# The down projection of a hybrid decoder block: weight operands streamed, their sums formed during gate and up, and a new order at the entry

## The chip, the cores and the metric

The program runs on one core of one Trainium2 chip, whose engines are TensorE (PE, its weight loads PEld), VectorE (DVE), ScalarE (ACT), GpSimd (POOL) and the DMA queues of SyncE (SP) and POOL. The metric is the device time of one execution in microseconds (us). The kernel before takes 1651.36 us, the median of three runs (1650.76 to 1653.76).

## The reference

One decoder block on a sequence of 1024 tokens of 1024 channels, float32. An attention branch and a retention branch read the same normed input, are merged by gates and projected; then a SwiGLU feed-forward with 2816 hidden channels. The change is in the feed-forward part:

```python
        mixed = jnp.sum(gates * u, axis=2).astype(x.dtype)
        x = x + jnp.einsum('bsd,de->bse', mixed, w_out[l])
        h = rms_norm(x, norm2_g[l])
        ff = jax.nn.silu(h @ ffn_w_gate[l]) * (h @ ffn_w_up[l])
        x = x + ff @ ffn_w_down[l]
```

## The kernel before, in words

**Arithmetic.** A matrix product is made in float32r from operands split into a high half (a copy by ACT, `ac`) and a low half (the rest, one subtraction on DVE, `tt`): three matmuls of 128x512 instead of one, high by high, high by low, low by high. `split`, `fill` and `d_fill` write such a pair.

**Seven products.** Gate and up (`ffn1`, line 1627) and down (`ffn2`, line 1855) are Winograd's form of Strassen's scheme: each operand is cut in 2x2 blocks, sums of blocks are formed, and seven block products, numbered 1 to 7, take the place of eight. In gate and up the moving side are the activations (`H`, and their three sums, split by `s_split` into `sh`), and the stationary side is one of 22 column blocks `f` of the weights G and U and their sums (`sums` and `late` in `fw_ops`, tiles `T`); a product `prod` is 12 matmuls. `SEQ` is the order of the 154 products. Their operands lie in 12 slots (`op_ring`), each freed by its product.

**Down.** Products 2, 1, 5, 6, 3, 7, 4 (`PLAN`) each run over 11 rows `k` of blocks, 12 matmuls a row, 924 in all. A-blocks are the feed-forward's activations, which gate and up write to memory, `f_scr`, one tensor for each `f` (`z3`, line 1703); B-blocks are rows of `ffn_w_down`. `d_first` (line 1760) loads: the two streams of product 2 go through a ring of six buffers (`st_ring`), the other six block matrices are loaded whole ("quads", `d_quad`) and stay. `d_s1`, `d_s2` and `d_ops` form eight sums of two SBUF tiles for each `k`, 88 in all, each by `both`: on POOL or on DVE, whichever the planner expects to end first. The split pairs go through a ring of eight operands (`dop_ring`), four rows' worth. `d_post` adds a product's bank to the residual.

**The entry.** Between the output projection and gate and up, `out_post` (line 1383) normalises each of eight token tiles `t`, transposes it on PE into two `psT` banks, and `h2_second` makes from these the split activations and the sums `sx`, for t from 4 to 7. `psT` is also the bank of product 5 (`z_ring2`).

**Order.** All of it is written as generators. A planner (`Sched.run`, line 168) takes step by step the instruction that could start first by its own cost figures, so each engine's queue is fixed when the program is built, and each queue runs strictly in order. A `Wait` of a generator holds back only its own later instructions.

Of the kernel before, what the change touches and what calls it, by code (L numbers as in the profile page):

```python
# [16 lines left out]
T = 1024  # L17
# [66 lines left out]
class Ring:  # L84
# [20 lines left out]
    def release(self, t):  # L105
        for e in self.live:
            if e[0] is t:
                e[1] = True
                return
        raise ValueError("not live")  # L110
# [101 lines left out]
def kernel(  # L212
# [1016 lines left out]
    big = es.enter_context(tc.tile_pool(name="big", bufs=1))  # L1229
# [153 lines left out]
    def out_post(t, o):  # L1383
# [17 lines left out]
        ps = []  # L1401
        for half in range(2):
            p = yield Alloc(t_ring)
# [6 lines left out]
        if t >= 4:  # L1410
            sch.spawn(h2_second(t, *ps), 1)
# [9 lines left out]
    def h2_second(t, p0, p1):  # L1421
# [8 lines left out]
        fl.add(("A2", 0, t))  # L1430
        yield Wait(lambda: all(("A1", half, t - 4) in fl for half in range(2)))
# [4 lines left out]
        t_ring.release(p0)  # L1436
        fl.add(("S", 1, t))
        yield from split(H[:, 0, t, 4:8, :], H[:, 1, t, 4:8, :], p1v)
        t_ring.release(p1)
# [25 lines left out]
    SEQ = [(1, 0), (2, 0), (1, 1), (2, 1), (5, 0), (6, 0), (6, 1), (7, 0), (5, 1), (4, 0), (3, 0), (7, 1)]  # L1465
# [23 lines left out]
    def op_views():  # L1489
# [15 lines left out]
        return Ring([wh(n) for n in range(4)] + [new(n) for n in range(8)], True)  # L1505
# [4 lines left out]
    def fw_ops():  # L1510
# [27 lines left out]
        def sums(f):  # L1538
            yield Wait(lambda: "fe" in fl and ("hx", NT - 1) in fl and ("G", f) in fl and ("U", f) in fl)
            if f == 1:  # L1540
                yield Wait(lambda: ("S", 0, NT - 1) in fl)
            G, U = fe["G", f][0], fe["U", f][0]
            a = yield Alloc(fe["T"])
            yield either(f)(a, U[:, 0:4], G[:, 0:4], ALU.subtract)
            b = yield Alloc(fe["T"])
            yield either(f)(b, U[:, 4:8], a, ALU.subtract)
            AB[f] = a, b
# [10 lines left out]
        AB = {}  # L1558
        for p, f in SEQ:
# [7 lines left out]
            if p in (5, 6) and f not in AB:  # L1567
                yield from sums(f)
            if p == 5:
                yield from put(f, 5, AB[f][0], lambda a=AB[f][0]: fe["T"].release(a))  # L1570
            elif p == 6:
                yield from put(f, 6, AB[f][1])
                sch.spawn(late(f, G, AB[f][1]), 2)
            elif p == 7:
                c = yield Alloc(fe["T"])
                yield either(f)(c, U[:, 4:8], U[:, 0:4], ALU.subtract)
                yield from put(f, 7, c, lambda c=c: fe["T"].release(c))
            elif p == 4:
                yield Wait(lambda: f in T4)
                yield from put(f, 4, T4[f], lambda f=f: fe["T"].release(T4[f]))  # L1580
            else:
                yield from put(f, 3, U[:, 4:8], drop("U", f))

# [84 lines left out]
    def c11(f, X):  # L1668
        yield Wait(lambda: ("y1", f) in fl and ("hx", NT - 1) in fl)
# [52 lines left out]
    KH = NF // 2  # L1722
    LAST = 3
    PLAN = [(2, "V"), (1, "Y"), (5, "V"), (6, "Y"), (3, "V"), (7, "Y"), (4, "V")]
    SRC = {1: ("A11", "B11"), 5: ("A21", None), 6: ("A11", "B11"), 3: (None, "B22"), 7: (None, "B12"), 4: ("A22", None)}
# [8 lines left out]
    def both(*a):  # L1734
        return Any(tt(*a, gp), tt(*a))

    def d_of(q, k):

        f, c = (int(q[2]) - 1 if q[0] == "A" else int(q[1]) - 1) * KH + k, int(q[1] if q[0] == "A" else q[2]) - 1
        c = slice(c * 512, c * 512 + 512)  # L1740
        return f_scr[f][:, c] if q[0] == "A" else ffn_w_down[0][f * 128:(f + 1) * 128, c]

    def st_make(n):
        def make():
            if n < 4:
                return flat(f2["raw"][n // 2])[:, n % 2 * 512:n % 2 * 512 + 512]
# [3 lines left out]
    def dop_make(n):  # L1750
        def make():
            if n < 4:
                return flat(f2["hl"][n // 2])[:, n % 2 * 1024:n % 2 * 1024 + 1024].rearrange("p (s t) -> p s t", s=2)
            return f2["op", n][:, 0:2]
# [5 lines left out]
    def d_first():  # L1760
        yield Wait(lambda: n_op[0] == 7 * NF and all((L1, p) in ops for p in (5, 6, 7)))
        f2["raw"] = [(yield Alloc(raw_ring)), (yield Alloc(raw_ring))]
        for k in range(2):
            yield from d_stream(2, k, "A12", gp)
            yield from d_stream(2, k, "B21", gp)
        for n, t in enumerate(fe["h"]):
            yield Wait(lambda: n_use[0] >= 7 * NF // 12 * 12 + 2 * n + 2)
            hl_ring.release(t)
# [228 lines left out]
```

## Time and profile before

| | us |
|---|---|
| three runs, median (lowest to highest) | 1651.36 (1650.76 to 1653.76) |
| the profiled execution | 1653.68 |
| its span, first to last instruction | 1652.0 |
| PE busy in the span | 1593.2 (96%) |
| DVE, ACT, POOL busy | 1067.0 (65%), 695.8 (42%), 321.3 (19%) |
| mean granted TensorE clock | 0.983 of full speed |

The profile is of one execution. PE is the engine whose idle time counts: the chain of work that ended last is PE for 75% of the span. Its idle time is short in sum, and lies in a few places; so the views to read are those that show a stretch of time, and not the sums over the span. Line 264 is the helper of every matmul, 284 of every ACT instruction, 294 of every two-operand DVE or POOL instruction, 318 of SP's DMAs and 317 of POOL's.

### The profile page before, as it was taken

The numbers are of one execution on the slowest core, as the hardware profiler recorded it, in microseconds if no ns is written. First come the engines' busy times: TensorE is split into PE (matmuls) and PEld (weight loads), VectorE is DVE, ScalarE is ACT, GpSimd is POOL, SyncE is SP. The second block draws the span as 40 slices with busy tenths as digits, with TensorE's granted clock in tenths as the row PEclk, the third lists the DMA queues.
The fourth block names the chain that finished last, engine by engine and source line by source line (L and its number), as shares of the span: only waits on it lengthen the run. The fifth ranks groups of instructions, "written<-read, shape, count | busy, mean of one in ns | idle before, by whom it ended". The sixth has DMA issues, their size and how long they took to land.

```text
span 1652.0 us, 23325 instructions
## 1 busy us (share of the span) xinstructions
PE 1593.2 (96%) x8404; PEld 1364.8 (83%) x8404; DVE 1067.0 (65%) x2681; ACT 695.8 (42%) x1413; POOL 321.3 (19%) x325
## 2 busy tenths in 40 slices
PE   7999999999999999999999998999999999897999
PEld 7999888888888888888888877888888888675887
DVE  7566578888779886524346578544455443498785
ACT  5233367666565565223115335333333332332442
POOL 2011212221103120000000002322332221036261
PEclk8999999999999999999999999999999999998999
DMA  6564221211421210233344323222222221882122
GB/s 181 139 179 132 62 61 59 65 42 42 114 75 52 55 49 23 62 108 115 109 130 137 112 87 90 94 85 88 80 88 77 85 69 51 304 314 71 32 90 83
DMA packets 158036, 160.71 MB, mean 97 GB/s; under 512 B 18400, under 2 KB 115680, under 8 KB 157664
## 3 DMA queue, kind: packets, MB, share of 16 engines
q1 hardware_dynamic: 152672, 147.68, 28.1%
q0 software_dynamic: 5248, 11.54, 2.5%
q8 instruction: 66, 1.08, 0.3%
q14 instruction: 50, 0.41, 0.1%
HBM read 120.38 MB, written 38.81 MB: 96 GB/s over the span
## 4 chain that ended last, share of the span: by engine, by line
PE 75%; DVE 6%; DMA 4%; issue 2%; POOL 1%; ACT 1%; SPq 0%; POOLq 0%; DVEq 0%; ACTq 0%
PE psF L264 25%; PE psS L264 23%; PE psO L264 12%; PE psT L264 11%; PE psT L269 4%; DVE P L1011 1%; PE psF L269 1%; DVE wh L294 1%; DVE P L299 1%; DVE pc L294 0%; DMA B__13707<-in_ffn_w_down_dram 0%; DMA B__13703<-in_ffn_w_down_dram 0%; DMA A__13653<-f_scr 0%; DVE sh L294 0%; DMA B__13711<-in_ffn_w_down_dram 0%
## 5 line engine op out<-in xcount | busy, mean ns | idle before, releaser
L264 PE MATMUL psF<-H,wh 128*128 128x512 f32 x1056 | 278.1, 396 | 2.1 <-ACT aw L284 2.1
L264 PEld LDWEIGHTS psF<-H,wh 128*128 128x128 f32 x1056 | 194.1, 189 | 36.6 <-ACT aw L284 2.5
L264 PE MATMUL psS<-H,zh 128*128 128x512 f32 x480 | 135.1, 405 | 0.3 <-ACT zs L284 0.3
L284 ACT ACTIVATE P<-P,pm 128x640 f32<-128x640 f32 (+7 forms) x128 | 93.9, 734 | 65.7 <-DVE pm L1011 64.4
L294 DVE TENSOR_TENSOR pT<-psT,pT 128x512 fp32r<-128x512 f32 (+1 forms) x152 | 92.4, 615 | 32.6 <-ACT pT L284 32.1
L284 ACT ACTIVATE pT<-psT 128x512 fp32r<-128x512 f32 (+1 forms) x152 | 79.0, 537 | 69.3 <-PE psT L269 68.7
L264 PE MATMUL psS<-kT,qt 128*128 128x384 f32 (+3 forms) x384 | 103.0, 343 | 1.9 <-DVE pm L1011 1.8
L294 POOL TENSOR_TENSOR T<-wraw 128x512 f32<-128x512 f32 x19 | 28.9, 1522 | 389.2 <-DVE op L294 389.2
L264 PEld LDWEIGHTS psS<-H,zh 128*128 128x128 f32 x480 | 85.9, 188 | 15.1 <-ACT zs L284 0.6
L264 PE MATMUL psO<-pT,vv 128*128 128x256 f32 x528 | 91.4, 289 | 3.7 <-DVE pT L294 3.6
L264 PE MATMUL psS<-whA,H 128*128 128x256 f32 (+1 forms) x672 | 91.7, 294 | 0.2 <-POOL whA L294 0.2
L284 ACT ACTIVATE wh<-wraw 128x1024 fp32r<-128x1024 f32 (+1 forms) x60 | 50.0, 841 | 97.4 <-PE psO L264 76.8
L264 PEld LDWEIGHTS psO<-pT,vv 128*128 128x128 f32 x528 | 79.5, 189 | 12.6 <-DVE pT L294 5.5
L294 DVE TENSOR_TENSOR wh<-wraw,wh 128x1024 fp32r<-128x1024 f32 (+1 forms) x60 | 60.7, 1016 | 42.0 <-ACT wh L284 40.7
L264 PEld LDWEIGHTS psS<-whA,H 128*128 128x128 f32 x672 | 87.1, 196 | 0.4 <-POOL whA L294 0.4
L294 DVE TENSOR_TENSOR op<-T,op 128x512 fp32r<-128x512 f32 x61 | 62.7, 1029 | 27.8 <-ACT op L284 27.4
L269 PE MATMUL psT<-ident,P 128*128 128x128 f32 x528 | 79.7, 273 | 0.1
L264 PEld LDWEIGHTS psS<-kT,qt 128*128 128x128 f32 x384 | 65.3, 189 | 10.2 <-DVE pm L1011 2.6
L264 PE MATMUL psS<-yt,wh 128*128 128x512 f32 x288 | 66.6, 389 | 0.0
L264 PE MATMUL psF<-sh,op 128*128 128x512 f32 x276 | 66.0, 389 | 0.0
L269 PEld LDWEIGHTS psT<-ident,P 128*128 128x128 f32 x528 | 61.9, 140 | 4.9 <-DVE P L299 0.8
L264 PE MATMUL psS<-wh 128*128 128x512 f32 x198 | 53.2, 409 | 11.7 <-DVE wh L294 11.4
(594 smaller groups left out, 3521.4 us busy)
## 6 DMA issues: line engine op xcount, KB each, us to landing
wraw<-in_w_in_dram SPq DMA_DIRECT2D x22, 512.0 KB, 4.1
f_scr<-fs SPq DMA_DIRECT2D x22, 512.0 KB, 2.6
qt<-q_scr POOLq DMA_DIRECT2D x16, 512.0 KB, 4.1
wraw<-in_ffn_w_gate_dram SPq DMA_DIRECT2D x12, 512.0 KB, 3.8
xx<-in_ffn_w_up_dram SPq DMA_DIRECT2D x12, 512.0 KB, 3.6
rawA<-in_w_in_dram SPq DMA_DIRECT2D x20, 256.0 KB, 3.5
zr<-in_w_in_dram SPq DMA_DIRECT2D x20, 256.0 KB, 3.4
z_scr<-zs SPq DMA_DIRECT2D x20, 256.0 KB, 2.1
```

Of the source, the lines that this page charges most:

```text
L264: lambda: pe.matmul(o, l, r, start=start, stop=stop, skip_group_check=True))
L269: return Op("pe", 109, 100, [o], [i], lambda: pe.transpose(o, i, ident))
L284: return Op("act", c, 150, outs, ins, lambda: act.activation(o, i, func, scale=scale, **kw))
L294: return vop(o, [a, b], lambda: (eng or dve).tensor_tensor(o, a, b, op), eng)
L299: return vop(o, ins, lambda: (eng or dve).tensor_scalar(o, a, s1, None, op0=op0), eng, fast)
L1011: lambda: dve.tensor_tensor_reduce(o, a, b, -sc, init, ALU.add, ALU.min, acc))
```

## The change

The helper lines move by 26. In words:

- **Sums in gate and up.** `wd_sums` loads, during gate and up, two rows of `ffn_w_down` at a time into a tile `row` (two DMAs of 512 KB on POOL's queue), forms the four sums T1 to T4 of the weight blocks in place on DVE (a wait counts the products done, `n_use`), and stores them to a scratch tensor `t_scr` in memory (two DMAs of 512 KB on POOL's queue). Eleven times. `row` takes the space of two of the twelve operand slots; ten stay in use after product 12 (`Slots`).
- **Streams.** In down all B operands, raw or summed, and A12 come through a ring of 24 buffers; only A11, A21 and A22 are loaded whole. The first four rows are loaded by POOL's queue while gate and up run. No sum in down goes to POOL; 44 sums are left there, all on DVE.
- **Operand ring.** Down's ring has ten operands (five rows), and they are gate and up's own slots: operand `n` may be filled once product 145 + n of 154 is done. For that the pool `big` is kept alive on the other side of SBUF.
- **Entry.** The last token tile is transposed into a `psS` and the `psO` bank; `h2_second` of t = 6 waits after its first part until t = 7 is normed; the sums of a column block are spawned apart; `c11` waits for ("sh", 0); product (5, 1) stands before (6, 1).

```diff
+class Slots(Ring):
+    def can(self):
+        return self.slot(self.n) not in self.held
...
-    big = es.enter_context(tc.tile_pool(name="big", bufs=1))
+    big = ctx.enter_context(tc.tile_pool(name="big", bufs=1, side="right"))
...
+        ring = t_ring if t < NT - 1 else ps_ring("SO")
         for half in range(2):
-            p = yield Alloc(t_ring)
+            p = yield Alloc(ring)
...
         fl.add(("A2", 0, t))
+        yield Wait(lambda: t != NT - 2 or ("hx", NT - 1) in fl)
         yield Wait(lambda: all(("A1", half, t - 4) in fl for half in range(2)))
         yield tt(s2, s1v, s3, ALU.subtract)
...
-        return Ring([wh(n) for n in range(4)] + [new(n) for n in range(8)], True)
+        return Slots([wh(n) for n in range(4)] + [new(n) for n in range(8)],
+                     lambda n: n if n < 12 else (0, 1, 2, 3, 6, 7, 8, 9, 10, 11)[(n - 12) % 10])
...
+    def wd_sums():
+        yield Wait(lambda: n_use[0] >= 12)
+        row = fe["pool"].tile([128, 4, 512], F32, name="row", tag="op")
+        a, b, c, d = [row[:, i] for i in range(4)]
+        for k in range(KH):
+            yield Wait(lambda: n_use[0] >= 12 + 13 * k)
+            for i in range(2):
+                f = i * KH + k
+                yield dma(row[:, 2 * i:2 * i + 2].rearrange("p a n -> p (a n)"),
+                          ffn_w_down[0][f * 128:(f + 1) * 128, :], gp)
+            for i, (o, x, y) in enumerate(((a, b, a), (b, d, b), (d, d, a), (c, c, d))):
+                yield Wait(lambda: n_use[0] >= 18 + i + 13 * k)
+                yield tt(o, x, y, ALU.subtract)
+            for i in range(2):
+                yield dma(t_scr[k][i], row[:, 2 * i:2 * i + 2].rearrange("p a n -> p (a n)"), gp)
+        fl.add("ts")
...
-        yield Wait(lambda: ("y1", f) in fl and ("hx", NT - 1) in fl)
+        yield Wait(lambda: ("y1", f) in fl and ("sh", 0) in fl)
...
-    st_ring = Ring([st_make(n) for n in range(6)], True)
-    dop_ring = Ring([dop_make(n) for n in range(8)], True)
+    st_ring = Ring([st_make(n) for n in range(NST)], True)
+    dop_ring = Ring([dop_make(n) for n in range(10)], True)
...
+    def d_loads():
+        yield Wait(lambda: ("U", L1) in fl)
+        f2["raw"] = []
+        for k in range(2, KH + 2):
+            if k < 6:
+                r = yield Alloc(raw_ring if k < 4 else fe["raw"])
+                f2["raw"].append(flat(r))
+            elif k == 6:
+                yield Wait(lambda: "pool" in f2)
+            yield from d_stream(2, k - 2, "A12", gp if k < 6 else None)
+            yield from d_stream(2, k - 2, "B21", gp if k < 6 else None)
+        for p, _ in PLAN[1:]:
+            for k in range(KH):
+                for q in {1: ("A11",), 5: ("A21", "A22")}.get(p, ()):
+                    yield dma(f2[q, k], d_of(q, k))
+                    dq[q, k] = f2[q, k]
+                if p == 3:
+                    yield from d_stream(3, k, "A12")
+                yield from d_stream(p, k, BQ[p])
...
+                if n < 10:
+                    yield Wait(lambda: n_use[0] >= 7 * NF - 9 + n)
```

What the change moves in the queues, at the three places that the prediction speaks of. First SP's queue where gate and up end: the last store of the feed-forward's activations (`f_scr_9876`) and the loads behind it, before (`f_scr_9868` is the A block of row 2):

```order
L318 DMA f_scr_9876<-fs 128x1024
L318 DMA st_13722<-f_scr_9868 128x512
L318 DMA st_13723<-in_ffn_w_down_dram 128x512
L318 DMA A_0__13700<-f_scr_9855 128x512
L318 DMA B_0__13701<-in_ffn_w_down_dram 128x512
L318 DMA wraw<-f_scr_9869 128x512
```

and now (`f_scr_9870` is the A block of row 4):

```order
L344 DMA f_scr_9876<-fs 128x1024
L344 DMA st_13772<-f_scr_9870 128x512
L344 DMA st_13773<-in_ffn_w_down_dram 128x512
L344 DMA st_13774<-f_scr_9871 128x512
L344 DMA st_13775<-in_ffn_w_down_dram 128x512
L344 DMA st_13776<-f_scr_9872 128x512
```

The first load behind the store serves row 4 instead of row 2, and product 2's streams follow each other without the whole blocks of product 1 between them.

Second, DVE's queue in down while the operands of the third product (5) are made, before (`wh` and `dop` are operand pairs, `tmp` a sum of B blocks, `xo` the residual):

```order
L294 TENSOR_TENSOR A_4__13708<-A_4__13656,A_4__13708 128x512
L294 TENSOR_TENSOR tmp<-B_4__13691,B_4__13709 128x512
L294 TENSOR_TENSOR B_4__13691<-B_4__13678,B_4__13691 128x512
L294 TENSOR_TENSOR xo<-xo,psT 128x512
L294 TENSOR_TENSOR wh<-tmp,wh 128x512
L294 TENSOR_TENSOR A_5__13710<-A_5__13657,A_5__13710 128x512
L294 TENSOR_TENSOR B_5__13692<-B_5__13679,B_5__13692 128x512
L294 TENSOR_TENSOR wh<-A_3__13655,wh 128x512
```

and now (`op` and `wh` are operand pairs, `st` a stream buffer):

```order
L320 TENSOR_TENSOR A_4__13803<-A_4__13803,A_4__13814 128x512
L320 TENSOR_TENSOR A_4__13792<-A_4__13803,A_4__13792 128x512
L320 TENSOR_TENSOR wh<-A_2__13801,wh 128x512
L320 TENSOR_TENSOR A_5__13804<-A_5__13804,A_5__13815 128x512
L320 TENSOR_TENSOR wh<-st_13775,wh 128x512
L320 TENSOR_TENSOR A_5__13793<-A_5__13804,A_5__13793 128x512
```

The sums of B blocks are gone; two sums of A blocks for each row stay.

Third, DVE's queue at the entry, from the norm of the last token tile, before (`hx` is the normed tile, `T` a sum of weights, `sx` a sum of activations, `fs` an output of gate):

```order
L304 SCALAR_TENSOR_TENSOR hx_10816<-xx,rs,g_9853 128x1024
L294 TENSOR_TENSOR T<-xx,wraw 128x512
L294 TENSOR_TENSOR sh<-sx,sh 128x2x384
L294 TENSOR_TENSOR fs<-psS,aw 128x512
L294 TENSOR_TENSOR T<-xx,T 128x512
...
L294 TENSOR_TENSOR op<-T,op 128x512
L294 TENSOR_TENSOR aw<-aw,psT 128x512
...
L294 TENSOR_TENSOR T<-wraw,T 128x512
L294 TENSOR_TENSOR H<-aw,H 128x512
L294 TENSOR_TENSOR sx<-aw,sx 128x4x128
```

and now:

```order
L330 SCALAR_TENSOR_TENSOR hx_10838<-xx,rs,g_9853 128x1024
L320 TENSOR_TENSOR T<-xx,wraw 128x512
L320 TENSOR_TENSOR sx<-aw,sx 128x4x128
L320 TENSOR_TENSOR sx<-sx,psT 128x4x128
L320 TENSOR_TENSOR op<-T,op 128x512
L320 TENSOR_TENSOR H<-psT,H 128x512
L320 TENSOR_TENSOR sx<-sx 128x4x128
L320 TENSOR_TENSOR aw<-aw,psO 128x512
L320 TENSOR_TENSOR sh<-sx,sh 128x2x384
L320 TENSOR_TENSOR H<-aw,H 128x512
```

The norm itself stands four instructions earlier (the four `sx` and `H` rows of tile 6, which now follow it), and the low half of tile 7's activations, `H<-aw,H`, is nine instructions behind the norm instead of eleven, with the two `fs` outputs of gate moved behind it.

## Rows read from the trace of the kernel before

**Rows 1.** Busy time by stretch: window length, then each engine's busy us (instructions), granted clock.

```profile
975.00:1030.00 55.00, 47.65 (x207) 38.75 (x206) 46.97 (x72) 29.65 (x51) 9.77 (x6) 0.94 0.32 96
1030.00:1395.00 365.00, 365.00 (x1612) 302.25 (x1611) 182.09 (x234) 132.97 (x229) 109.24 (x77) 1.00 0.25 80
1408.50:1647.95 239.45, 221.12 (x924) 178.40 (x922) 178.53 (x216) 87.28 (x150) 86.49 (x55) 0.95 0.42 153
```

**Rows 2.** PE's waits from 1395 us to the end: us, times, longest.

```profile
PE psS L264 <- DVE wh L294: 11.4, 4, 7.4
PE psS L264 <- issue: 3.3, 1, 3.3
PE psS L264 <- ACT dop L284: 2.1, 1, 2.1
PE psS L264 <- DVE dop L294: 0.9, 1, 0.9
...
PE psF L264 <- DVE wh L294: 0.4, 1, 0.4
```

**Rows 3.** Timeline where down begins: start us, us, engine, line, [idle before <- releaser].

```profile
1395.58 14.90 SPq L318 DMA_DIRECT2D f_scr<-fs  x2
1409.45 0.69 DVE L294 TENSOR_TENSOR fs<-fs,u 128x512 f32<-128x512 f32 x1
1412.81 0.32 SPq L318 DMA_DIRECT2D st<-f_scr  x1
1415.77 1.36 ACT L284 ACTIVATE dop<-st 128x512 fp32r<-128x512 f32 x2 [9.18 <-DMA st<-f_scr]
1417.24 4.46 PE L264 MATMUL psS<-dop,dop 128*128 128x512 f32 x9 [3.34 <-issue]
```

**Rows 4.** Timeline in the third product of down.

```profile
1498.69 1.74 DVE L294 TENSOR_TENSOR A__13714<-A__13659,A__13714 128x512 f32<-128x512 f32 x1
1499.85 1.70 POOL L294 TENSOR_TENSOR A__13716<-A__13660,A__13716 128x512 f32<-128x512 f32 x1
1500.36 1.74 DVE L294 TENSOR_TENSOR wh<-tmp,wh 128x512 fp32r<-128x512 f32 x1
1502.15 3.78 PE L264 MATMUL psS<-wh 128*128 128x512 f32 x8 [7.38 <-DVE wh L294]
1512.28 0.69 DVE L294 TENSOR_TENSOR tmp<-B__13698,B__13719 128x512 f32<-128x512 f32 x1
```

**Rows 5.** Timeline at the entry, 978 to 1024 us.

```profile
978.75 1.06 ACT L284 ACTIVATE hx<-xx 128x1024 f32<-128x1024 f32 x1
980.75 0.14 DVE L300 TENSOR_SCALAR ss<-ss 128x1 f32<-128x1 f32 x1
982.01 0.14 DVE L334 TENSOR_SCALAR nw<-ss 128x1 int32<-128x1 int32 x1
984.13 1.28 DVE L304 SCALAR_TENSOR_TENSOR hx<-xx,rs,g 128x1024 f32<-128x1024 f32 x1
987.34 1.68 PEld L264 LDWEIGHTS psS<-H,wh 128*128 128x128 f32 x8
993.90 0.68 DVE L294 TENSOR_TENSOR sx<-sx,psT 128x512 f32<-128x512 f32 x1
994.73 5.29 PE L264 MATMUL psT<-H,op 128*128 128x512 f32 x12 [5.29 <-DVE sx L294]
1010.78 2.88 PE L264 MATMUL psF<-H,op 128*128 128x512 f32 x12
1023.89 3.01 PE L264 MATMUL psF<-H,wh 128*128 128x512 f32 x12 [2.07 <-ACT aw L284]
```

**Rows 6.** DVE and POOL groups by line, 1040 to 1380 us: busy us, mean ns | idle before.

```profile
L294 DVE TENSOR_TENSOR op<-T,op 128x512 fp32r<-128x512 f32 x49 | 52.5, 1070 | 25.7 <-ACT op L284 25.4
L294 DVE TENSOR_TENSOR op<-xx,op 128x512 fp32r<-128x512 f32 x18 | 12.3, 686 | 18.9 <-ACT op L284 18.9
L294 POOL TENSOR_TENSOR T<-xx,T 128x512 f32<-128x512 f32 x18 | 26.1, 1453 | 118.7 <-DVE op L294 65.5 <-DVE wh L294 52.4
L317 POOL DMA_DIRECT2D wraw<-f_scr x2 | 1.2, 583 | 0.0
```

**Rows 7.** DMA: a stretch of loads in down, columns as rows 1, last GB/s; issues to landing (us).

```profile
1432.00:1460.00 28.00, 24.56 (x98) 19.05 (x97) 19.47 (x26) 11.28 (x20) 6.29 (x4) 0.94 1.05 403
...
qt<-q_scr POOLq DMA_DIRECT2D x16, 512.0 KB, 4.1
...
f_scr<-fs SPq DMA_DIRECT2D x22, 512.0 KB, 2.6
...
wraw<-f_scr POOLq DMA_DIRECT2D x2, 256.0 KB, 3.7
```

More of the change, by code (lines that the diff above doesn't have):

```diff
@@ L108, in release, with __init__, alloc @@
                 e[1] = True
+                return
+        raise ValueError("not live")
+class Slots(Ring):
+    def __init__(self, makers, slot):
+        self.makers, self.slot, self.n, self.held = makers, slot, 0, {}
+        self.was = {}
+    def can(self):
+        return self.slot(self.n) not in self.held
+    def alloc(self, sched):
+        i = self.slot(self.n)
+        seed = sched.last_use(self.was[i], True) if i in self.was else 0.0
+        t = self.held[i] = self.was[i] = self.makers[i]()
+        self.n += 1
+        sched.seed[key(t)] = seed
+        return t
+    def release(self, t):
+        for i, e in self.held.items():
+            if e is t:
+                del self.held[i]
                 return
@@ L1556, in either @@
             return both if f > 1 else tt
-        AB = {}
+        T1, T2, read, made = {}, {}, set(), set()
         for p, f in SEQ:
@@ L1566, in fw_ops @@
             U = fe["U", f][0]
-            if p in (5, 6) and f not in AB:
-                yield from sums(f)
+            if p in (5, 6) and f not in made:
+                made.add(f)
+                sch.spawn(sums(f), 2)
             if p == 5:
-                yield from put(f, 5, AB[f][0], lambda a=AB[f][0]: fe["T"].release(a))
+                yield Wait(lambda: f in T1)
+                yield from put(f, 5, T1[f], lambda f=f: drop_a(f))
             elif p == 6:
-                yield from put(f, 6, AB[f][1])
-                sch.spawn(late(f, G, AB[f][1]), 2)
+                yield Wait(lambda: f in T2)
+                yield from put(f, 6, T2[f])
+                sch.spawn(late(f, G, T2[f]), 2)
             elif p == 7:
+                yield Wait(lambda: f in T2)
                 c = yield Alloc(fe["T"])
@@ L1582, in fw_ops @@
                 yield from put(f, 3, U[:, 4:8], drop("U", f))
+    KH = NF // 2
+    t_scr = [[dram.tile([128, T], F32, name=f"t_scr{k}_{i}") for i in range(2)] for k in range(KH)]
+    def wd_sums():
[14 more added lines that the diff above has]
+        fl.add("ts")
     def a_op(p, s, k):
@@ L1789, in d_stream, with d_sums @@
         dq[q, p, k] = r
[L1791 to L1795 removed]
+    def d_sums():
         for k in range(KH):
             yield Wait(lambda: ("A21", k) in dq and ("A22", k) in dq)
[L1798 removed]
+            yield tt(f2["A21", k], f2["A21", k], f2["A22", k], ALU.add)
             fl.add(("S1", k))
[L1801 to L1804 removed]
+            yield Wait(lambda: (1, k, 0) in dop)
+            yield tt(f2["A11", k], f2["A21", k], f2["A11", k], ALU.subtract)
@@ L1933 @@
     sch.spawn(s_split(), 1)
-    sch.spawn(d_first(), 3)
+    sch.spawn(wd_sums(), 4)
+    sch.spawn(d_loads(), 3)
     sch.spawn(d_ops(), 3)
     sch.spawn(ffn2(), 6)
-    sch.run(lambda: "ffn1" in fl and all(("F", f) in fl for f in range(NF)))
+    sch.run(lambda: "ffn1" in fl and "ts" in fl and all(("F", f) in fl for f in range(NF)))
     fes.close()
```

140 lines of the change are left out of this document (46 added, 94 removed).

## The prediction

> **What bounds the kernel now.** I read the span by stretches first. In gate and up, 1030 to 1395 us, PE is busy for the whole stretch of 365.00 us with 1612 matmuls at full granted clock [rows 1]: one costs 365.00/1612 = 0.2264 us, a product of 12 costs 2.72 us, and nothing but fewer matmuls could shorten that stretch. The reader should see there too that DVE is busy for 182 us of it and POOL for 109 us: room that costs nothing as long as PE never waits. The other two stretches of the group are not full. Down's 924 matmuls are worth 924 x 0.2264 = 209.2 us at the steady rate, but the stretch is 239.45 us. So down loses 30.2 us: 239.45 - 221.12 = 18.3 us idle, and 11.9 us of matmuls that ran long at a granted clock of 0.95 on average. The entry, 975 to 1030 us, has 55.00 - 47.65 = 7.35 us idle, at a clock of 0.94.
>
> Next, what ended PE's waits in down [rows 2]: 11.4 us for low halves that DVE writes into `wh`, the longest 7.4 us; then "issue" 3.3 us and `dop` 2.1 and 0.9 us. Two places make up nearly all of it.
>
> The first is the beginning of down [rows 3]. The last store of the activations sits on SP's queue for 14.90 us, since its data come only with DVE's last `fs`, at 1409.45 to 1410.14. Behind it in the same queue stands the load of row 2; it is issued at 1412.81, ACT gets its data at 1415.77, and PE, which had only two rows in hand, has run dry. The second is the third product of down [rows 4]. The sums of blocks run on POOL and DVE at once, and while they overlap one takes 1.70 us on POOL and 1.74 us on DVE; alone on DVE it takes 0.69 us. DVE falls behind, PE waits 7.38 us for one operand, and its next 8 matmuls take 3.78 us instead of 1.81: after a wait the clock is granted low. That is where the 11.9 us went.
>
> At the entry [rows 5] product 5 uses the `psT` banks, which also carry the transposes of the last token tile; it waits 5.29 us until DVE's `sx<-sx,psT` (993.90, 0.68 us) has read the bank, and then takes 5.29 us instead of 2.72.
>
> **The change part by part. Down's beginning.** PE now starts with four rows of product 2 in hand, 4 x 2.72 = 10.9 us of work, to about 1419.4. Row 4 is the first that comes by the load behind the last store. If the store issues at 1410.5 as before and the load right behind it takes as long as before from issue to ACT (1415.77 - 1412.81 = 2.96 us) [rows 3], its split is done at 1410.5 + 2.96 + 0.65 for the second block + 0.63 for ACT + 0.69 for DVE = 1415.4 or a little later. If the load is issued 2.3 us after the store, as before, it is 1417.7. Both lie ahead of 1419.4, by 4.0 and 1.7 us. The wait goes; late next is row 5, 2.72 us later, with a load of its own close behind, so nothing is.
>
> **Down's third product.** All sums of B blocks leave down (88 sums become 44), and POOL makes none, so DVE should run at 0.69 us an operation instead of a mixture: some 223 operations of this size by the program, 223 x 0.69 = 154 us of 209, where it was 178.5 us before [rows 1]. From the first streamed fill at about 1414, the last operand of the third product is DVE's 88th operation: 1414 + 88 x 0.69 = 1475. PE needs it 32 products after 1408.5, at 1495.5. Slack 20 us. If the contention stayed, at 1.74 us, it would be 1567 and 72 us late; but its cause, sums on POOL beside it, is gone by the order of the queues. With no wait there is no low clock behind one. Taken together down can give back between 14 us (the beginning, and half of the third product with its slow matmuls) and all 30.2. I take **29.0**: the operations' slack points at nearly all, and I leave 1.2 us for the first matmuls and small waits of 0.3 to 0.5 us as in [rows 2].
>
> **The entry.** By hand through the queues: DVE's small operations for the norm end about 0.8 us earlier (`ss` at 980.75 now), the norm of tile 7 begins 1.8 us earlier, near 982.3, since four rows of tile 6 stand behind it, and its transposes go into a `psS` and the `psO` bank. So `psT` is free of tile 7, and product 5 is held only by `H<-aw,H`, near 989.3; it loses the 5.29 us wait. But product (6, 0), and behind it the rest, now waits for `sh` 0, whose last pieces I put at 994.9 on DVE, with about 2.85 us of wait, and (5, 1) for its operand until about 999.3. The two products that follow end near 1007.5; the same work before ended at 1010.78 [rows 5], where `psF<-H,op` begins. So **3.3** us are gained. The bounds: nothing, if the new waits are as long as the old; and 5.29 + 2.07 + (5.29 - 2.72) = 9.9 us, if every wait and slow matmul of the stretch goes. The wait of 2.07 us at 1021.8 for `aw` is left as it is in the forecast. I take the small value since I can name the wait that takes the other's place.
>
> **Gate and up.** Added are 44 sums on DVE, at 0.69 us [rows 4] to 1.77, and 44 DMA issues on POOL. Rows of this stretch bear on both [rows 6]: DVE operations of this size average 686 ns in one group and 1070 ns in the group that meets POOL's sums, and POOL issues a DMA in 583 ns. That is 44 x 0.69 to 44 x 1.77 = 30 to 78 us on DVE on top of 182 of 365, and 44 x 0.58 = 26 us on POOL on top of 109. Both stay below 365; POOL's sums had 118.7 us of idle time ahead of them. What covers it is a queue of operands made in advance: ten slots instead of twelve, 27 instead of 33 us of PE's work. If that cover were gone, each of eleven groups of sums could cost the excess of one collided sum, 11 x (1.77 - 0.69) = 12 us. I take 0, since PE waits for nothing over 365 us with twelve slots, and DVE's own wait there is for ACT. The DMA queues: 22 loads and 22 stores of 512 KB, 23 MB, over 365 us of 80 GB/s; a stretch of down ran at 403 GB/s [rows 7], so there is room. They stand on POOL's queue, behind which only POOL's own sums wait; SP's queue loses them. In down 124 loads of 256 KB on SP replace 103, at 403 GB/s 0.65 us each, 81 us of 209.
>
> **The sum.** 29.0 + 3.3 + 0 = 32.3 us, taken from the profiled execution's 1653.68: 1621.4. That execution is 2.3 us above the median shown, so 1619.1 against the median; I say **1620**. By the bounds: from 9.9 + 30.2 = 40.1 us gained, 1611, to 14 + 0 - 12 = 2 us, 1649. About 0.2% (3.3 us) is what a measurement of this kernel can tell from no change.
>
> **The rivals.** *All of it goes* (0.07). Every wait of the entry and of down goes, `aw` included, since DVE and ACT get the lead they lacked: 1651.4 - 40 = 1612, with 1611 as the floor. Against it stands the wait for `sh` 0 that the new order writes itself.
>
> *DVE is still the bound of the third product* (0.10). Two sums of A blocks for each row stay and now are all DVE's; if 15 of the 29 us stay as waits or as a low clock: 1635. For it speaks that DVE is busy for 154 of 209 us and is due early in that stretch; against it 20 us of slack.
>
> *Streamed loads come one at a time* (slower, 0.02). Down now lives on 124 loads of 256 KB. The place is SP's queue; the point from which it decides is 209/124 = 1.69 us a load. If each took the 2.96 us of the load in [rows 3] with none beside it, down would last 124 x 2.96 = 367 us, 158 more than PE needs, and the time would be 1620 + 158 = 1778. Against it: pieces of this size already ran at 403 GB/s [rows 7], 0.65 us each, because many are in flight, and a ring of 24 buffers keeps them so.
>
> The Trainium skill, on its page "DMA: Bandwidth & Descriptors", section "Bandwidth", speaks against this change: DMAs are to be batched to 1 MiB or more for 75% of peak. By the fit of the section "Anatomy of one DMA", a fixed 2.0 us and then 436 GB/s, I estimate 2.6 us for 256 KB and 322 us for 124 in series, and 1733 us for the kernel. The trace agrees for a single load (2.96 us) and not for a train of them (0.65 us).
>
> *Sums wait for their loads* (slower, 0.04). In gate and up DVE's queue is strictly in order. Each group of sums waits there for a load that POOL's queue issues six products, 16.3 us, earlier. If it lands later, DVE stands still, and behind it the operations that empty PSUM for PE, about one product of 2.72 us ahead. So it costs PE from a landing 19.0 us after the issue on, and eats the whole gain from 19.0 + 32.3/11 = 21.9 us on; at 25 us it costs 11 x 6.0 = 66 us, 1686. Against it: loads of 512 KB on that queue landed 4.1 us after their issue, one of 256 KB 3.7 us [rows 7].
>
> *Waits only move* (0.03). Down's late operand is late for another reason, such as the ring's order, and comes out where it was: 1651, no change. That the sums do leave down is plain from the queues, so I give it little.
>
> **How the numbers follow.** The forecast has 0.74; its own range is 1615 to 1627 (the entry between 0 and 9, down between 26 and 30.2). Range **1611 to 1634**: it holds the forecast, the first rival and the nearer half of the second; outside remain 0.05 of the second, 0.09 of the last three, and some 0.04 of the forecast's tails. Faster: 0.74 + 0.07 + 0.10 = 0.91; same 0.03; slower 0.02 + 0.04 = 0.06.
>
> **What would show it.** Right: PE's idle time from 1395 us on falls from some 18 us to under 3, and down's 924 matmuls run at full granted clock in about 210 us; no wait for `wh` of more than a microsecond; POOL has no sums in down and DVE's operations there average near 0.69 us; gate and up still have PE busy for the whole stretch; at the entry the wait for `sx` is gone, and one for `sh` of 2 to 3 us stands in its place. Wrong: waits for `st` loads through down (loads one at a time), for `row` in DVE's queue in gate and up, a DVE mean above 1 us in down, or PE's waits for `op` in gate and up, where ten slots would not be enough.

## The result and the profile after

The changed kernel takes 1629.62 us (median of 4 runs, 1624.83 to 1629.82), the kernel before in the same comparison 1652.56 us (4 runs, 1650.76 to 1654.45). The ratio is 0.9854, 95% interval 0.9832 to 0.9876: 22.9 us faster, clear of noise. The forecast was 1620 with a range of 1611 to 1634. So the direction and the range held, and 9 us of the promised 32 are missing. The profiled execution spans 1628.1 us, 23.9 less than before.

The windows of the changed kernel by stretch, columns as in [rows 1] (after the length: PE, its weight loads, DVE, ACT and POOL, then the granted clock, the DMA share and GB/s); its down begins 1 us later on the span's clock:

```profile
975.00:1030.00 55.00, 52.41 (x228) 41.89 (x226) 48.87 (x78) 32.56 (x54) 13.31 (x10) 0.97 0.40 125
1030.00:1395.00 365.00, 365.00 (x1584) 296.77 (x1583) 214.79 (x277) 131.82 (x227) 114.30 (x111) 1.00 0.41 139
1409.50:1624.20 214.70, 212.76 (x924) 174.08 (x922) 139.60 (x223) 84.88 (x146) 0.00 (x0) 0.99 0.54 192
```

Down went from 239.45 to 214.70 us, with 1.9 us idle. In the entry's 55 us PE is busy for 52.41 us instead of 47.65. The line to stop at is the second. PE is busy for 365.00 of 365.00 us, as in [rows 1], and the granted clock is 1.00 in both; but it makes 1584 matmuls where it made 1612. A busy share of 100% hides that each matmul became longer: 0.2304 us instead of 0.2264.

PE's waits from 1395 us to the end of the changed kernel, the answer to [rows 2]:

```profile
PE psF L290 <- ACT op L310: 1.5, 1, 1.5
PE psF L290 <- ACT aw L310: 1.0, 1, 1.0
PE psF L290 <- DVE op L320: 0.4, 1, 0.4
```

The 11.4 us for `wh` and the 3.3 us of "issue" are gone. Down's beginning in the timeline, the answer to [rows 3] (columns as there):

```profile
1411.16 0.32 SPq L344 DMA_DIRECT2D f_scr<-fs  x1
1413.80 0.32 SPq L344 DMA_DIRECT2D st<-f_scr  x1
1417.35 1.15 ACT L310 ACTIVATE wh<-st 128x512 fp32r<-128x512 f32 x2 [9.76 <-DMA st<-f_scr]
1418.01 1.29 DVE L320 TENSOR_TENSOR wh<-st,wh 128x512 fp32r<-128x512 f32 x2 [6.88 <-ACT wh L310]
1419.52 0.85 PE L290 MATMUL psO<-op 128*128 128x512 f32 x3
1420.21 2.23 PE L290 MATMUL psS<-wh 128*128 128x512 f32 x9
```

Row 4's load is issued 2.3 us after the store, and DVE ends its fill at 1419.30. PE takes it up at 1420.21, straight after row 3, with 0.9 us to spare.

The entry, the answer to [rows 5], PE alone:

```profile
976.07 2.89 PE L290 MATMUL psF<-H,wh 128*128 128x512 f32 x12
987.85 2.88 PE L290 MATMUL psT<-H,op 128*128 128x512 f32 x12
991.35 0.49 PE L290 MATMUL psF<-sh,op 128*128 128x512 f32 x1 [0.39 <-DVE op L320]
993.88 3.89 PE L290 MATMUL psF<-sh,op 128*128 128x512 f32 x10 [2.03 <-DVE sh L320]
1006.61 2.96 PE L290 MATMUL psF<-H,op 128*128 128x512 f32 x12
1017.73 2.88 PE L290 MATMUL psF<-H,wh 128*128 128x512 f32 x12
```

Product 5 has no wait ahead of it. The wait of 2.03 us for `sh` 0 stands in its place, behind one of 0.39 us for an operand (`op`), and the wait of 2.07 us for `aw` ahead of the fourteenth product is gone.

Three landmarks divide the span in every profile: the first matmul of gate and up, the first of its fourteenth product, and the place where gate and up's last product ends and down runs on. Before they lie at 977.50, 1023.89 [rows 5] and 1408.52 us; in the changed kernel at 976.07, 1017.73 and 1409.51. Down then ends 239.3 and 214.5 us later, its last matmul counted at the steady spacing. The stretches, each read from one profiled execution, are steadier than whole times: the time ahead of the first landmark alone lies between 971.3 and 979.4 us in the kernels below, though no edit is aimed at anything there.

| kernel | entry | gate and up | down | median us |
|---|---|---|---|---|
| before | 46.4 | 384.6 | 239.3 | 1652.56 |
| changed | 41.7 | 391.8 | 214.5 | 1629.62 |
| 1: pad of 32 bytes | 43.1 | 387.3 | 214.5 | 1625.32 |
| 2: pad of 64 bytes | 43.5 | 392.4 | 213.3 | 1627.37 |
| 3: ACT's fills in order | 41.7 | 391.8 | 213.1 | 1629.74 |
| 4: the old entry | 46.5 | 391.9 | 213.4 | 1633.71 |
| 5: pad of 224 bytes | 42.1 | 385.1 | 211.8 | 1621.81 |
| 6: before, tiles shifted | 46.0 | 391.7 | 238.6 | 1662.64 |
| 7: before, sums on DVE | 45.5 | 384.6 | 232.8 | 1643.89 |
| 8: late rows | 41.7 | 391.2 | 213.0 | 1626.20 |
| 9: pad and two orders | 42.7 | 385.1 | 215.5 | 1624.40 |
| 10: pad, entry, late rows | 42.7 | 384.5 | 213.5 | 1618.50 |
| 11: pad of 96 bytes (one execution) | 41.7 | 391.7 | 212.2 | 1628.41 |
| 12: sums on POOL | 41.7 | 391.8 | 212.9 | 1627.94 |

From before to the changed kernel the 23.9 us are: entry 4.7, gate and up -7.2, down 24.8, and 1.4 ahead of the entry, which lies within its scatter, with 0.1 behind down.

### The profile page after: what moved, and what is told of

It reads as the page before. It is cut to its first block, busy times and chain, and to the rows that moved or that the text cites. A ratio compares the mean times of both kernels' runs of the same rounds, so it can differ in the third digit from the quotient of the medians.

```text
span 1628.1 us, 23458 instructions
## 1 busy us (share of the span) xinstructions
PE 1590.0 (98%) x8404; PEld 1358.4 (83%) x8404; DVE 1069.5 (66%) x2746; ACT 696.8 (43%) x1413; POOL 244.0 (15%) x308
## 4 chain that ended last, share of the span: by engine, by line
PE 82%; DVE 5%; issue 0%; ACT 0%; DMA 0%; DVEq 0%; ACTq 0%
PE psF L290 26%; PE psS L290 26%; PE psO L290 13%; PE psT L290 12%; PE psT L295 4%; DVE P L1037 1%; PE psF L295 1%; DVE P L325 1%; DVE pc L320 0%; DVE pT L320 0%; DVE sx L320 0%; DVE T L320 0%; DMA k_scr<-ks 0%; DVE sh L320 0%; DVE y L320 0%
## 5 line engine op out<-in xcount | busy, mean ns | idle before, releaser
L320 DVE TENSOR_TENSOR wh<-wraw,wh 128x1024 fp32r<-128x1024 f32 (+1 forms) x55 | 55.9, 1018 | 37.7 <-ACT wh L310 37.5
L290 PEld LDWEIGHTS psS<-yt,wh 128*128 128x128 f32 x288 | 54.1, 188 | 11.2
L310 ACT ACTIVATE op<-T 128x512 fp32r<-128x512 f32 x55 | 34.6, 630 | 63.3 <-PE psT L290 35.7
L320 DVE TENSOR_TENSOR op<-T,op 128x512 fp32r<-128x512 f32 x55 | 51.3, 936 | 15.9 <-ACT op L310 15.1
```

Of the source, the lines that this page charges most:

```text
L290: lambda: pe.matmul(o, l, r, start=start, stop=stop, skip_group_check=True))
L310: return Op("act", c, 150, outs, ins, lambda: act.activation(o, i, func, scale=scale, **kw))
L320: return vop(o, [a, b], lambda: (eng or dve).tensor_tensor(o, a, b, op), eng)
```

## The experiments

### Why gate and up became slower: runs 1, 2, 5, 6 and 11

The timeline of PE in the changed kernel, in the middle of gate and up:

```profile
1203.17 2.96 PE L290 MATMUL psT<-H,op 128*128 128x512 f32 x12
1205.97 2.96 PE L290 MATMUL psO<-sh,op 128*128 128x512 f32 x12
1208.77 2.88 PE L290 MATMUL psF<-H,wh 128*128 128x512 f32 x12
1211.49 2.88 PE L290 MATMUL psO<-H,wh 128*128 128x512 f32 x12
```

Products whose weights lie in an `op` slot start 2.80 us apart (2.80/12 = 0.233 us a matmul), products with weights in `wh` 2.72 us, as all of them did before. In the built programs `wh`, `H` and `sh` begin at addresses that are multiples of 256 in both kernels; the three `op` tiles in the pool `big` did too, and now, at the other side of SBUF, they begin at 204768, 212960 and 221152, that is 224 behind a multiple of 256. Before, the fourth `op` tile lay at 220928, as far out as any now, at full speed. The first edit is an unused tile ahead of the pool:

```diff
+    ctx.enter_context(tc.tile_pool(name="pad", bufs=1, side="right")).tile([128, 8], F32, name="pad")
     big = ctx.enter_context(tc.tile_pool(name="big", bufs=1, side="right"))
```

> In the changed kernel matmuls that take their weights from an `op` slot follow each other in gate and up every 0.233 us, those with `wh` every 0.227 us as before. Three of the four `op` tiles now begin 32 bytes behind a multiple of 64. Here an unused tile of 32 bytes moves them to a multiple of 64. Theory (offset): the `op` matmuls go back to 0.227 us, gate and up lose some 7 us, row changes in down another 1: 1621.5 us (1620 to 1623). Rival (place or traffic: the far end of SBUF, or the added DMA bytes of 139 instead of 80 GB/s slow the loads of weights): 0.233 us and 1629.6 us stay.

Gate and up took 387.3 us: better than 391.8, not the 385 of the theory. `op` products now start 2.75 us apart. Run 2 is the same with 16 elements (64 bytes).

> The same with 64 bytes, so that the tiles move but stay 32 bytes behind a multiple of 64. Theory (offset): `op` matmuls every 0.233 us, 1629.6 us as in the changed kernel. Rival (any shift of the tiles against H changes it): another spacing than 0.233 us, and 1621 to 1628 us.

Gate and up took 392.4 us, as the offset theory has it. So it isn't any shift, but a multiple of 64 is not enough. Run 5 uses 56 elements (224 bytes), by which the tiles come to multiples of 256.

> With 32 bytes of padding the `op` matmuls came every 0.229 us instead of 0.233, with 64 bytes every 0.233 as without; `wh`, H and `sh` all begin at multiples of 256. Here 224 bytes put the `op` tiles on multiples of 256 too. Theory (offset, and 64 bytes are not enough): 0.227 us as in the kernel before, gate and up 7 us shorter than in the changed kernel: 1622.3 us (1620.5 to 1624). Rival (the rest is the place, or the added DMA traffic): 0.229 us stay, 1625.3 us.

The median is 1621.81 us (1618.63 to 1621.97), 0.9820 of before (0.9795 to 0.9845); every run lies below every run of the changed kernel. PE's timeline in gate and up of this kernel:

```profile
1201.51 2.88 PE L290 MATMUL psT<-H,op 128*128 128x512 f32 x12
1204.23 2.88 PE L290 MATMUL psO<-sh,op 128*128 128x512 f32 x12
1206.95 2.88 PE L290 MATMUL psF<-H,wh 128*128 128x512 f32 x12
```

All products are 2.72 us apart again, and gate and up takes 385.1 us. With all the sums and DMAs that the change adds still there, it is 0.4 us behind the kernel before, and 0.5 of that is a wait for `aw` that grew from 0.5 to 1.0 us. So the work that the change moved into gate and up costs half a microsecond at most, and the place of the tiles cost 6.7 us.

Run 11 asks whether multiples of 128 do (24 elements).

> 96 bytes of padding: the `op` tiles begin at multiples of 128, and not of 256. With 224 bytes (multiples of 256) `op` matmuls came every 0.2267 us. Theory (128 is enough): 0.2267 us in gate and up, which then takes 385.1 us from its fourteenth product to its end. Rival (it takes 256): 0.228 to 0.233 us, 386.5 to 392 us.

391.7 us: they do not. The five offsets behind a multiple of 256, by the mean spacing of `op` matmuls in gate and up: 0: 226.7 ns; 128: 232.6; 160: 233.3; 192: 228.9; 224: 233.2.

Run 6 puts the fault into the kernel before, with none of the change's traffic, and asks which side has to be off.

```diff
+    es.enter_context(tc.tile_pool(name="pad", bufs=1)).tile([128, 8], F32, name="pad")
     big = es.enter_context(tc.tile_pool(name="big", bufs=1))
```

> The kernel before, with 32 bytes ahead of the pool that holds the operand tiles: `op` and `sh` now begin 32 bytes behind a multiple of 64, `wh` and H do not. Traffic and work are those of the kernel before. Theory (weights off a multiple): H,op and sh,op come every 0.233 us, H,wh and sh,wh every 0.227: 7 us slower, 1658.7 us. Rival (moving and weights off by different amounts): H,op and sh,wh are slow, sh,op and H,wh are not: some 5 us slower. Rival (place or traffic): all stay at 0.227 us and 1651.7 us.

PE's timeline of this kernel in gate and up; `op` and `sh` are 32 bytes off here, `H` and `wh` are not:

```profile
1202.84 2.96 PE L264 MATMUL psS<-H,op 128*128 128x512 f32 x12
1205.64 2.89 PE L264 MATMUL psT<-sh,op 128*128 128x512 f32 x12
1208.36 2.88 PE L264 MATMUL psO<-sh,op 128*128 128x512 f32 x12
```

and further on:

```profile
1222.23 2.90 PE L264 MATMUL psS<-H,wh 128*128 128x512 f32 x12
1224.97 2.97 PE L264 MATMUL psT<-sh,wh 128*128 128x512 f32 x12
1227.78 2.49 PE L264 MATMUL psF<-sh,wh 128*128 128x512 f32 x10
```

By its pattern this is the first of the two rivals: `sh,op`, both off by the same, run 2.72 us apart, and `H,op` and `sh,wh`, off by different amounts, 2.80. It costs more than the 5 us put on it. The same shows in the changed kernel's down, where weights and moving data both come from operand slots: at 1414.76 and 1417.48 us two rows of the same kind stand 2.72 us apart. By the profiled executions the kernel became 7.8 us slower (span 1659.8 against 1652.0), 7.1 of them in gate and up. The medians lie 11.3 apart (1662.64 and 1651.33 in that comparison). The difference is one of executions: the profiled one of the kernel before (1653.68) lies 2.3 us above that median, the one of run 6 (1661.55) 1.1 us below its own.

### What made down faster: runs 7, 8 and 12

Run 7 takes one of the two suspected causes out of the kernel before.

```diff
     def both(*a):
-        return Any(tt(*a, gp), tt(*a))
+        return tt(*a)
```

> The kernel before, with all 88 sums of down on VectorE and none on GpSimd. Theory (contention: sums on both engines at once stretch one another to 1.7 us): DVE's operations in down take 0.69 us, PE's waits for `wh` (11.4 us) and the low clock behind them shrink to under a third: 1640 us or less. Rival (the amount of work: 88 sums beside the fills are too many for the third product): up to 1500 us DVE has 16 operations more, 103 x 0.69 = 71 us against 68 before, so it is late as before: 1649 to 1655 us.

Both were half right. Down took 232.8 us instead of 239.3, the median 1643.89 us (ratio 0.9955, 0.9941 to 0.9969). A group of DVE's operations in down, and the two longest of PE's waits from 1395 us on:

```profile
L294 DVE TENSOR_TENSOR wh<-tmp,wh 128x512 fp32r<-128x512 f32 x11 | 7.6, 690 | 4.0 <-ACT wh L284 3.9
```

```profile
PE psS L264 <- DVE wh L294: 6.5, 4, 4.2
PE psS L264 <- issue: 3.6, 1, 3.6
```

The contention is gone (in the kernel before the mean of this group was 1173 ns), and yet PE waits 6.5 of the 11.4 us. So POOL's part in the sums cost 6.5 us of down, and not all of it.

Run 12 puts the contention back into the changed kernel: `tt(..., gp)` for its four kinds of A sums, so that DVE has no sums in down at all, and POOL 44.

> The changed kernel, with its 44 sums of A blocks in down on GpSimd instead of VectorE. Theory (both contention and the amount of work made the third product late; with the B sums gone there is slack): DVE's operations beside POOL's sums stretch again, their mean in down rises from 0.69 to over 0.8 us, but PE waits little more: down 214 to 219 us (214.5 now), 1629 to 1634 us. Rival (contention alone was the cause): a wait of several us comes back in the third product, down over 222 us, 1637 us or more. Rival (no contention, VectorE only had too much work): mean 0.69 us, down at most 214.5 us.

A group of DVE's operations and a window of this kernel in down:

```profile
L320 DVE TENSOR_TENSOR op<-st,op 128x512 fp32r<-128x512 f32 x37 | 35.6, 980 | 3.5 <-ACT op L310 3.5
```

```profile
1450.00:1500.00 50.00, 50.00 (x222) 41.19 (x221) 49.92 (x39) 21.33 (x38) 44.12 (x27) 1.00 0.80 294
```

DVE is busy for 49.92 of 50 us with 39 instructions, its mean in down is 0.87 us, and PE waits in down as in the changed kernel, 1.5 and 0.4 us: down takes 212.9 us, under the 214 to 219 of the theory. The Trainium skill, on its page "GPSIMD Engine Reference", section "1. Specifications", says that GpSimd shares its SBUF interfaces with VectorE and contends with its instructions of two SBUF inputs; these runs agree (980 against 687 ns for the same group). The cost is hidden by a lead, and it is nearly used up. The tightest row of the third product, by DVE's last half of a row and PE's start on that row, first in the changed kernel (row 3, counted from 0), then in run 12 (row 6):

```profile
1472.49 0.69 DVE L320 TENSOR_TENSOR wh<-st,wh 128x512 fp32r<-128x512 f32 x1
1477.73 2.20 PE L290 MATMUL psS<-wh 128*128 128x512 f32 x9
```

```profile
1482.12 1.78 DVE L320 TENSOR_TENSOR op<-st,op 128x512 fp32r<-128x512 f32 x1
1484.96 2.20 PE L290 MATMUL psS<-op 128*128 128x512 f32 x9
```

The lead is 4.6 us in the first and 1.1 us in the second. So contention alone does not bring the wait back, and without contention 88 sums with a ring of eight operands still wait. What took away the rest of the wait can be the smaller number of sums, the longer ring of ten operands or the new order of the loads; no run changes one of them alone, so their shares are not shown.

Run 8 takes two of the four prepared rows away.

```diff
+            if k == 4:
+                yield Wait(lambda: ("F", L1) in fl)
-            yield from d_stream(2, k - 2, "A12", gp if k < 6 else None)
-            yield from d_stream(2, k - 2, "B21", gp if k < 6 else None)
+            yield from d_stream(2, k - 2, "A12", gp if k < 4 else None)
+            yield from d_stream(2, k - 2, "B21", gp if k < 4 else None)
```

> The changed kernel, with only two rows of product 2 loaded during gate and up instead of four; the loads of rows 2 and 3 stand behind the last store on SP's queue. Theory (the rows in hand took away the wait at down's beginning): PE runs dry after 2 x 2.72 us, waits 3 to 4 us, and runs 3 us longer at the low clock: 1636 us (1634 to 1639). Rival (the ring of 24 buffers did it): the wait stays away, 1629.6 us.

```profile
1408.78 0.84 PE L290 MATMUL psO<-op 128*128 128x512 f32 x3
1411.41 0.50 PE L290 MATMUL psS<-op 128*128 128x512 f32 x1 [1.80 <-ACT op L310]
1412.14 1.21 PE L290 MATMUL psS<-op 128*128 128x512 f32 x4 [0.22 <-DVE op L320]
```

The wait came back where it was expected, at 1.8 and 0.2 us instead of 3 to 4, and in this execution no low clock followed (granted clock 1.00 from 1410 to 1418 us). The time did not rise, since the planner now orders the fills of product 6 otherwise, and the waits of 1.5 and 0.4 us there are gone. The prepared rows are worth some 2 us here, and nearly 4 where the low clock follows: behind the same wait run 10 was granted 0.76 from 1405 to 1412 us, and nine matmuls took 1.6 us longer in all. The expected 6 us were too many.

### The wait that is left in down, and the entry: runs 3, 4, 9 and 10

ACT's timeline in the changed kernel, around PE's last wait:

```profile
1510.51 0.63 ACT L310 ACTIVATE op<-A__13796 128x512 fp32r<-128x512 f32 x1 [1.60 <-PE psT L290]
1513.23 0.63 ACT L310 ACTIVATE op<-A__13797 128x512 fp32r<-128x512 f32 x1 [1.56 <-PE psT L290]
1514.29 0.61 ACT L310 ACTIVATE op<-wraw 128x512 fp32r<-128x512 f32 x1
```

```profile
1514.95 0.49 PE L290 MATMUL psF<-op 128*128 128x512 f32 x1 [1.53 <-ACT op L310]
1517.21 2.76 PE L290 MATMUL psT<-op 128*128 128x512 f32 x6
```

The last row is at the lower of the two clocks, 1.2 GHz (427 ns a matmul). Run 5 has the same wait of 1.53 and 0.40 us, and the same six matmuls behind it take 1.54 us instead of 2.76:

```profile
1511.34 1.54 PE L290 MATMUL psT<-op 128*128 128x512 f32 x6
```

So the same wait does not always bring the low clock. With it the granted clock over 8 us around the wait was 0.79 in the changed kernel and in run 1, and 1.00 in runs 2, 4, 5, 11 and 12, one profiled execution each. That is 1.6 us by which rows of the table differ in down, and no edit is shown to be the cause.

The fill `op<-wraw` belongs to row 5 of product 6, which PE is waiting for. It stands behind the fills of rows 6 to 9, and these wait for slots that PE frees one row at a time. ACT waits for no DMA there: the block had been loaded long before, and the planner's costs put it late. Run 3 holds ACT's halves of the fills to the ring's order.

```diff
-                sch.spawn(d_fill(p, k, b, o, src, then), 2)
+                sch.spawn(d_fill(p, k, b, o, src, then, n - 1, n_fill), 2)
-    def d_fill(p, k, b, o, src, then):
+    def d_fill(p, k, b, o, src, then, m, n_fill):
+        yield Wait(lambda: n_fill[0] == m)
         yield ac(o[:, 0], src)
+        n_fill[0] += 1
```

> Down's one remaining wait of 1.5 and 0.4 us on PE (product 6, row 5) is for a fill that stands nine places too late in ACT's queue. Here the fills' ACT halves are held to the order of the ring. Theory (ACT's order): the wait and the low clock behind it go, 1.9 + 1.7 = 3.6 us less: 1626.0 us. Rival (the streamed block of that row lands late): ACT stands at that fill, the fills behind it are late too, and the time is 1629.6 us or more.

The wait for ACT is gone, and a new one has come, for DVE's half of another row. PE's waits from 1030 us on:

```profile
PE psF L290 <- DVE wh L320: 1.6, 1, 1.6
PE psF L290 <- ACT aw L310: 1.0, 1, 1.0
PE psS L290 <- DVE wh L320: 0.5, 1, 0.5
```

1629.74 us: that is the rival's time and not its reason, since none of these waits is for a streamed block. The wait moved to the next queue that is out of order. Run 4 undoes the entry.

```diff
-        ring = t_ring if t < NT - 1 else ps_ring("SO")
+        ring = t_ring
...
-        yield Wait(lambda: t != NT - 2 or ("hx", NT - 1) in fl)
...
-    SEQ = [(1, 0), (2, 0), (1, 1), (2, 1), (5, 0), (6, 0), (5, 1), (7, 0), (6, 1), (4, 0), (3, 0), (7, 1)]
+    SEQ = [(1, 0), (2, 0), (1, 1), (2, 1), (5, 0), (6, 0), (6, 1), (7, 0), (5, 1), (4, 0), (3, 0), (7, 1)]
...
-            yield Wait(lambda: f == 0 or ("sh", 0) in fl)
+            if f == 1:
+                yield Wait(lambda: ("S", 0, NT - 1) in fl)
...
-            yield Wait(lambda: ("A2", 0, NT - 1) in fl)
...
-        yield Wait(lambda: ("y1", f) in fl and ("sh", 0) in fl)
+        yield Wait(lambda: ("y1", f) in fl and ("hx", NT - 1) in fl)
```

> The changed kernel with the entry's order undone: the last token tile is transposed into psT, (6, 1) stands before (5, 1), and the added waits on the norm and on `sh` 0 are gone. By the prediction 3.3 us come back: 1632.9 us. By the trace of the changed kernel, where the fourteenth product of gate and up starts 6.2 us earlier than before: 1635.8 us. Rival (the gain is taken back behind the entry): 1629.6 us.

```profile
993.60 5.33 PE L290 MATMUL psT<-H,op 128*128 128x512 f32 x12 [5.29 <-DVE sx L320]
1022.91 3.02 PE L290 MATMUL psF<-H,wh 128*128 128x512 f32 x12 [1.71 <-ACT aw L310]
```

1633.71 us (1632.89 to 1634.43), 4.1 us above the changed kernel; by the stretch 46.5 against 41.7 us. Both of the entry's old waits are back, the one for `aw` too.

Run 9 has the pad of 224 bytes, `sh` 0 ahead of tile 7's last split and of T4 (two waits for ("sh", 0)), and whole fills in order (`yield from d_fill(...)` in place of the spawn). Run 10 has the pad, the same entry, and run 8's late rows.

> Padding of 224 bytes, and two orders: at the entry the low half of `sh` 0 is written ahead of the last split of token tile 7 and of T4, and in down both halves of a fill are held to the ring's order on ACT and on DVE. Theory (each wait left is one misplaced instruction): the wait for `sh` 0 shrinks from 2.0 us to under 0.5, the waits of 1.5 and 0.4 us in product 6 go, with 1.5 us of low clock each: 1621.8 - 2 - 1.5 - 2 - 1.5 = 1615 us (1613 to 1618). Rival (the wait moves to the next operand, as it did when only ACT's halves were held in order): 1619 to 1623 us.

> Padding of 224 bytes, `sh` 0 first at the entry, and as in the run with late rows only two rows of product 2 loaded during gate and up. That run had a wait of 2.0 us at down's beginning, and none in product 6; down took 213.0 us instead of 214.5, and the padding takes 2.8 us from it. Theory: down 210.5 us, entry 2 to 3.5 us less: 1617.5 us (1615.5 to 1619.5). Rival (with rows back at full speed PE runs dry sooner, the wait at the beginning grows by what the padding gave): 1620 us or more.

Run 9 was 1624.40 us (1621.25 to 1625.62), slower than the pad alone and just above the rival's range: the rival by its mechanism. The longest of its waits of PE from 975 us on:

```profile
PE psT L290 <- ACT op L310: 2.4, 1, 2.4
PE psS L290 <- ACT wh L310: 2.0, 1, 2.0
PE psF L290 <- DVE wh L320: 1.5, 1, 1.5
PE psF L290 <- ACT aw L310: 1.0, 1, 1.0
PE psT L290 <- DVE op L320: 0.9, 1, 0.9
```

The wait for `sh` is gone, and (5, 1), the next product, waits 2.4 and 0.9 us for its operand. The slot of this operand is the tile of the first `sx`, which tile 7's last piece still reads, and that piece was put back; ACT's timeline has it:

```profile
994.20 0.63 ACT L310 ACTIVATE op<-T 128x512 fp32r<-128x512 f32 x1 [3.02 <-DVE sx L320]
```

In down two waits of 2.0 and 1.5 us replace one. Run 10 had 1618.50 us (1616.74 to 1626.49), ratio 0.9803 (0.9778 to 0.9828). Its entry has the same moved wait (42.7 us, no gain where 2 to 3.5 us were expected), and down took 213.5 us instead of 210.5, so its theory was wrong on both terms, and that the median lies in its range is luck. The profiled execution came to the first landmark at 971.7 us, run 5's at 977.2; over the three stretches run 10 takes 1.7 us more than run 5. Its interval overlaps that of run 5, and its runs scatter more, so the medians don't settle which of the two is faster. Both beat the changed kernel in the median; run 5 is the one with a single edit and a reason that is shown.

## Why the prediction was right, and where its sum was off

Direction and range held, the forecast did not: 1629.62 lies outside its own range of 1615 to 1627. It falls into 1611 to 1634 because that was widened for half of the second rival, which did not come; the loss that filled the place was on no list. To that extent the range held by luck.

**Down's beginning** was right in place and kind: the load 2.3 us behind the store was the case of the two that came, the slack 0.9 us where 1.7 was worked out, and the wait went.

**Down's third product** was right in the outcome: no wait for `wh`, no sum on POOL, no operation of DVE much above 0.69 us, 139.6 us of DVE in down where 154 were forecast (operations standing back to back start 0.60 us apart, though each lasts 0.69). The reason was half wrong: "its cause, sums on POOL beside it, is gone" names the contention, and run 7 gives that 6.5 us alone, while run 12 has it back at no cost in time. What is left is 44 sums instead of 88, together with the longer ring and the new order of the loads. The "slack 20 us" was wrong as well: it lets DVE run on to 1475 us, but a fill needs a slot that PE has freed, and the ring holds five rows. DVE ended the last operand of the third product at 1487.9 us, PE took it at 1496.9, and the least lead of that product was 4.6 us.

**Down's size** was 29.0 us and measured 24.8. The step that failed is "I leave 1.2 us for the first matmuls and small waits": some 5.3 us were lost. One misplaced fill cost 1.9 us of waiting on PE and some 0.5 us around it; in the profiled execution a low clock followed (7 matmuls of 427 instead of 227 ns, 1.6 us with the slow ones beside them); and rows that change between `wh` and `op` lost about a microsecond to the offset of the tiles. "With no wait there is no low clock behind one" stands; but behind a wait the low clock came in some executions and not in others.

**The entry** was 3.3 us and measured 4.7 by its stretch, 4.1 by run 4. The wait for `sh` 0 came where it was put, 2.0 us against 2.85. At `psF<-H,op` (1006.61 us), the place for which the 3.3 us were worked out, 2.7 were gained beyond the 1.4 ahead of the entry. Too careful was "the wait of 2.07 us at 1021.8 for `aw` is left as it is": it belonged to the old order and went with it.

**Gate and up** is the term that failed. "I take 0, since PE waits for nothing over 365 us" held to the letter, PE waits for nothing now too. The sentence had no place for matmuls that take longer without a wait, and the bound of 12 us was put on the DVE sums, which cost half a microsecond at most. The move of `big` to the other side of SBUF was told in the change and priced nowhere. Gate and up lost 7.2 us: 6.7 are the spacing of the matmuls, 0.5 a longer wait for `aw` at the end. With the tiles put back to multiples of 256 (run 5) the forecast of 1620 meets 1621.8; its terms don't, since the entry gave 4.3 and down 27.5.

**The rivals.** DVE was not the bound of the third product. The streamed loads did not come one at a time: down moved 192 GB/s over its whole length, and no wait of PE there is for a DMA. The rule of the Trainium skill on batching (page "DMA: Bandwidth & Descriptors", section "Bandwidth") did not decide here; 256 KB pieces in a ring of 24 buffers kept up with PE. The fit that the prediction took from this page of the Trainium skill (section "Anatomy of one DMA") is told there for DMAs that GpSimd issues. These loads stand on SP's queue, so the measured 2.96 us is the figure for a single one. No instruction of DVE in gate and up waited for the loads of `row`; POOL issued them 13 products apart, and their median landing was 5.7 us against the 16.3 us allowed. That waits only move came in small: the wait of 1.9 us in product 6 is one of the ring's order.

## What to carry to other kernels

When a change moves a buffer, write down the start addresses of the weights and of the moving data of each matmul before and after, modulo 256, and give them the same remainder (0 with 0 and 32 with 32 were the two tried); an unused tile of a few bytes does it. Where an engine is 100% busy, compare the count of instructions in a stretch of equal length, not the busy time. Where a wait is one misplaced instruction in a queue, mending that queue alone tends to show the next one: runs 3 and 9 moved waits and gained nothing, nor did the entry of run 10.

## What was not expected of the hardware

Matmuls of 128x512 at full granted clock follow each other every 226.7 ns when weights and moving data start at the same remainder of 256 bytes, and every 229 to 233 ns at the four other remainders tried, with no wait, no lower clock and no longer weight load in the trace (187 to 189 ns in both kernels). A remainder of 64 less than a multiple (192) costs a third of what 224, 160 and 128 cost. It was seen for fp32r operands with one of the sides at a multiple of 256, and for both off by 32 alike, where nearly nothing is lost. What in the chip makes it is open: the runs show where it is and that a pad removes it, not how it comes about.

The same wait of PE, 1.53 and 0.40 us, was followed by matmuls at 427 ns in two of seven profiled executions, and by none in the other five. What decides it is open too.
